# A streaming encoder layer: x arrives transposed, its split carries the norm's weight, and the row roots are applied where products leave PSUM

## The chip, the core and the metric

One core of one Trainium2 chip runs the whole layer. The metric is device microseconds (us) of one execution. Engines are named as in the profile: PE (matmuls), PEld (its weight loads), ACT (ScalarE), DVE (VectorE), POOL (GpSimd), and SP, whose queue issues all transfers.

## The reference, cut to what matters

```python
def rmsnorm(x, g):
    return x * lax.rsqrt(jnp.mean(x * x, -1, keepdims=True) + EPS) * g

def layer_inputs(x, norm_g, w_in, b_gate, qn_g, kn_g):      # x: 2048 prompt rows, and 64 sample rows
    h = rmsnorm(x, norm_g) @ w_in                           # (rows, 1024) @ (1024, 6144)
    qa, ka, va, za, qb, kb, vb, zb, ga, gb = split(h)       # ten column blocks
    qa, ka = rmsnorm(qa per 64, qn_g), rmsnorm(ka per 64, kn_g)
    ...
```

After it come differential attention over chunks (for the sample rows over a cache of 4096 frames), a retention branch, gates, three more projections and the residual add. Everything is fp32 in and out, and keys, values and states are outputs too.

Two facts make the change possible. The root of the norm is one factor per row of x, so it can be taken after the product: (r · x · g) @ W = r · ((x · g) @ W). And a product that is normalised again (qa, ka) loses the factor r anyway, if the eps in the second norm is scaled by 1/r².

## The kernel before

**Precision.** Each fp32 operand is split into a high and a low part in a rounded format (`xh`, `xl` for x, `wh`, `wl` for weights), and a product is three matmuls: high·high, high·low, low·high.

**Stages.** x is worked in two halves of 1024 prompt rows. Of a half, `xh` and `xl` hold the transposed, normalised x in two segments (tiles `xh0`/`xl0` and `xh1`/`xl1`) of 512 columns; the second segment of half 0 has 64 columns more for the sample rows. The contraction of 1024 is eight chunks of 128. `w_stream` walks over the column blocks of `w_in`: in half 0 the values (`va`), keys and queries, each as one group of 512 columns, then 256-column groups of the retention inputs and gates. Blocks that are needed with rows on partitions come from `natural` (x is the stationary operand); those needed transposed from `transposed` (the weights are). A coroutine per product (`fin_va`, `fin_qk`, `fin_vb`, `fin_t`) empties its PSUM bank.

**Order.** The code is a small planner. Coroutines with priorities yield until a planned PE time or until a buffer is free, and so fix the order in which PE, ACT and DVE get their instructions; projections fill the time in which attention waits. Each engine runs its queue strictly in that order. POOL and SP are ordered by the compiler's scheduler. SP has at most eight transfers in flight: each waits for the one eight before it.

**x before.** `x_prep` loads 128 rows of x as one tile `xt` of 128x1024. ACT squares and sums a row (L329), ACT and DVE form the inverse root (L335 to L350), and DVE multiplies the tile with the root and with the norm's weight row (L359). That row is spread over the partitions by a matmul with ones (`spread`, L308) in half 0 and by a transfer in half 1. `x_tile` then transposes the tile: eight 128x128 transposes on PE (L389) into two banks (`tp`, `pv`), a high part by ACT (L396) and a low part by DVE (L397). There are 17 such tiles. `opening` mixes the first of them with the first product by the list `OPENING` (matmuls of L578), and the others between the chunks of the values' group (L520, and L516 for the sample rows).

**Weights.** A piece is loaded to `ws`, ACT makes `wh` (L474), POOL makes `wl` (L484), for three early pieces DVE does (L481).

Of the kernel before, what the change touches and what calls it, by code (L numbers as in the profile page):

```python
# [43 lines left out]
XFLY = (3, 5)  # L44
# [4 lines left out]


OPENING = [(k[0], int(k[1])) for k in ("H0 X0 H1 X1 H2 X2 L0 H3 X3 L1 H4 X4 L2 T1 H5 X5 L3 H6 X6 L4 "
                                       "H7 X7 L5 L6 L7").split()]
# [12 lines left out]
class Hybrid:  # L65
    def __init__(self, tc, ins, outs):
        self.tc = tc
        self.nc = tc.nc
        self.i = ins
        self.o = outs  # L70
        self.pe = self.act = self.dve = self.pool = self.dma = 0.0
        self.tasks = []
        self.seq = 0
        self.res = {k: Res(n) for k, n in BUFS.items()}
        self.res["row"] = Res(ROWS)
        self.live = {"z": 0, "w": 0, "r": 0, "m": 0}
        self.done = set()
# [61 lines left out]
    def ld(self, dst, src, nbytes=0):  # L139
        self.nc.sync.dma_start(dst, src)  # L140
        self.dma = max(self.dma, self.pe) + nbytes / 300.0
        return self.dma + DMA_LAT
# [31 lines left out]
    def consts(self):  # L174
# [6 lines left out]
        yield lambda: len(self.xt_ready) > 8  # L181
# [34 lines left out]
        le = c("le", [128, 2])  # L216
        nc.scalar.activation(le, ls, AF.Exp)
        lam = c("lam", [128, 1])
# [43 lines left out]
    def x_prep(self, half):  # L262
        self.xq = []
        self.xin = []
        self.xfly = 0
        gn = jk = tg = None
        if half:
            yield from self.take("row", 2)
            gn, jk = self.row("gn"), self.row("xjk")
        else:  # L270
            yield from self.take("row")
            jk = self.row("xjk")
        tiles = self.xtiles(half)
        left = [len(tiles)]
        for j, (src, r, seg, col) in enumerate(tiles):
            yield lambda: self.xfly < XFLY[half] and (half > 0 or j < 2 or self.wloads >= 8)
            self.xfly += 1
            yield from self.take("row")
            xt = self.row("xt")[:r]
            self.xq.append(None)  # L280
            tx = self.ld(xt, src, 4096 * r)
            if j == 0 and half == 0:
                yield from self.take("row")
                gz = self.row("gz")
                self.nc.vector.memset(gz[:, :512], 0.0)
                self.nc.gpsimd.memset(gz[:, 512:], 0.0)
                tg = self.ld(gz[0:1, :], self.i["norm_g"][0:1, :], 4096)
                self.ld(self.ident, self.i["c_ident"], 1 << 16)
                gn = [self.psum("s") for _ in range(2)]
                self.gz = (gz, tg)  # L290
            elif j == 0:
                tg = self.ld(gn, self.i["norm_g"][0].partition_broadcast(128), 1 << 19)
            self.xin.append([xt, jk, gn, tx, tg, r, seg, col, left])
            if half:
                self.spawn(self.x_norm(j), 1, "w")
            yield self.pe
        yield lambda: left[0] == 0
        if half == 0:
            self.give("s", self.dve + LAT, 2)
        self.give("row", self.dve + LAT, 1 + half)  # L300

    def spread(self):

        gz, t = self.gz
        self.until(t)
        for k, ps in enumerate(self.xin[0][2]):
            yield from self.take("s")
            self.nc.tensor.matmul(ps, self.ones, gz[:, 512 * k:512 * k + 512], start=True, stop=True)  # L308
            t = self.P(2048)
        self.give("row", t)  # L310
        self.warm(2)
        self.xin[0][4] = t
# [10 lines left out]
    def norm_sums(self, j):  # L323

        nc = self.nc
        xt, jk, gn, t, tg, r, seg, col, left = self.xin[j]
        st = self.sp.tile([128, 3], F32, tag="x_st", name="x_st")
        ss, ms, y = (st[:r, k:k + 1] for k in range(3))
        nc.scalar.activation(jk[:r], xt, AF.Square, accum_out=ss)  # L329
        self.xin[j] += [ss, ms, y, self.A(1024, max(self.pe, t), 190)]  # L330

    def norm_log(self, j):
        nc = self.nc
        ss, ms, y, t = self.xin[j][9:]
        nc.scalar.activation(y, ss, AF.Ln, scale=1.0 / D, bias=self.epst[:y.shape[0]])  # L335
        nc.scalar.activation(y, y, AF.Exp, scale=-0.5)
        self.A(1, 0, 100)
        self.xin[j].append(self.A(1, 0, 40))

    def norm_mean(self, j):  # L340
        ss, ms, y, t = self.xin[j][9:13]
        self.nc.vector.tensor_scalar(ms, ss, 1.0 / D, EPS, op0=ALU.mult, op1=ALU.add)
        self.V(100, t)

    def norm_root(self, j):
        nc = self.nc
        ss, ms, y, t, t2 = self.xin[j][9:]
        nc.vector.tensor_scalar(ms, y, y, ms, op0=ALU.mult, op1=ALU.mult)
        nc.vector.tensor_scalar(ms, ms, -0.5, 1.5, op0=ALU.mult, op1=ALU.add)
        nc.vector.tensor_scalar(y, y, ms, 128.0 if isinstance(self.xin[j][2], list) else 1.0,  # L350
                                op0=ALU.mult, op1=ALU.mult)
        for _ in range(3):
            self.V(60, t2)

    def norm_scale(self, j):
        xt, jk, gn, tx, tg, r, seg, col, left, ss, ms, y, t, t2 = self.xin[j]
        for k, g in enumerate(gn if isinstance(gn, list) else [gn]):
            sl = slice(512 * k, 512 * k + g.shape[1])
            self.nc.vector.scalar_tensor_tensor(out=xt[:, sl], in0=xt[:, sl], scalar=y, in1=g[:r],  # L359
                                                op0=ALU.mult, op1=ALU.mult)  # L360
        self.xq[j] = (xt, self.V(1300, max(t2, self.xin[0][4])), r, seg, col)
        left[0] -= 1

    def x_norm(self, j):
        yield self.xin[j][3]
        self.norm_sums(j)
        self.norm_log(j)
        ss, ms, y, t, t2 = self.xin[j][9:]
        yield t
        self.norm_mean(j)  # L370
        yield t2
        self.norm_root(j)
        if self.xin[0][4] > self.pe:
            yield self.xin[0][4]
        self.norm_scale(j)

    def x_tile(self, j, wait=True, mid=None):
        nc = self.nc
        yield lambda: len(self.xq) > j and self.xq[j] is not None
        xt, t, r, seg, col = self.xq[j]  # L380
        if wait:
            yield t
        self.until(t)
        for q in range(2):
            tag = "tp" if q == 0 else "pv"
            yield from self.take(tag)
            tp = self.psum(tag)
            for c in range(4):
                nc.tensor.transpose(tp[:, c * r:(c + 1) * r],  # L389
                                    xt[:, (4 * q + c) * 128:(4 * q + c + 1) * 128],  # L390
# [1834 lines left out]
```

## Time and profile before

| | |
|---|---|
| time, three runs | 1954.27, 1958.63, 1959.08 us (median 1958.63) |
| the profiled execution | 1957.16 us, its span 1955.4 us, granted TensorE clock 0.997 |
| PE busy | 1936.0 us, 99% of the span |
| DVE, ACT, POOL busy | 1068.5, 1021.7, 476.0 us (55%, 52%, 24%) |
| moved by DMA | 303.86 MB, 155 GB/s in the mean |
| first product's first matmul | at 10.10 us |
| first matmul of the second column group (keys) | at 68.06 us |

The page gives busy times of one execution. In a row of the timeline stand the start, the busy time (the time over all, where x2 or more were merged), the engine, the line, the operation and its shape; in brackets is the idle time before it and what ended that. Matmuls overlap in the pipeline, so the distance of two starts, and not the busy time of one, says what a matmul costs PE.

### The profile page before, as it was taken

Reading aid. Unit: us, or ns where it says so; the run is one execution under the profiler, and the core shown is the slowest. Engines: PE = TensorE matmul, PEld = TensorE weight load, DVE = VectorE, ACT = ScalarE, POOL = GpSimd, SP = SyncE. Lnnn points to the kernel's source line nnn. Section 1 sums busy time; section 2 is a strip of 40 time slices with the busy share of each in tenths; the row PEclk is TensorE's granted clock in tenths of the full one; section 3 lists DMA queues with packets and bytes.
Section 4 is the critical chain, followed back from the end, with each engine's and each line's share of the span. In section 5 each row is a group of like instructions: output and inputs, shape, how many; then the busy total and the mean of one; then the engine's idle time right before and its main releaser. Section 6 shows DMA issues by size and latency. Waiting matters only on the chain.

```text
span 1955.4 us, 34054 instructions
## 1 busy us (share of the span) xinstructions
PE 1936.0 (99%) x12070; PEld 1740.5 (89%) x12070; DVE 1068.5 (55%) x2642; ACT 1021.7 (52%) x2220; POOL 476.0 (24%) x427
## 2 busy tenths in 40 slices
PE   9999999999999999999999999999999999999999
PEld 7878999999988989999998888888888899998887
DVE  6553665535565326546857656634753257545653
ACT  6432776645544436435766656644763545653321
POOL 2310211212121221222111211121122355543422
PEclk9999999999999999999999999999999999999999
DMA  7647554335656756664343342462233668866651
GB/s 250 210 130 197 150 162 116 119 86 159 181 162 170 174 137 209 197 202 136 111 130 95 103 136 83 130 182 91 73 98 111 208 201 261 258 197 196 189 156 59
DMA packets 367917, 303.86 MB, mean 155 GB/s; under 512 B 75137, under 2 KB 332417, under 8 KB 367746
## 3 DMA queue, kind: packets, MB, share of 16 engines
q1 hardware_dynamic: 367746, 301.68, 52.5%
q8 instruction: 95, 1.56, 0.3%
q14 instruction: 76, 0.62, 0.1%
HBM read 196.40 MB, written 100.14 MB: 152 GB/s over the span
## 4 chain that ended last, share of the span: by engine, by line
PE 91%; DVE 3%; DMA 3%; ACT 1%; issue 1%; SPq 1%; POOL 1%; ACTq 0%; DVEq 0%; POOLq 0%
PE mm L520 53%; PE mm L1882 4%; PE s L1000 3%; PE s L1001 3%; PE at L1108 3%; PE at L1882 2%; PE pv L1088 2%; PE pv L1087 2%; PE pv L1086 2%; PE mm L1670 1%; PE mm L1672 1%; PE mm L1671 1%; PE s L1671 1%; PE s L1672 1%; PE s L1670 1%; PE s L1882 1%
## 5 line engine op out<-in xcount | busy, mean ns | idle before, releaser
L520 PE MATMUL mm<-xh,wh 128*128 128x512 f32 (+2 forms) x1280 | 459.1, 359 | 0.0
L484 POOL TENSOR_TENSOR wl<-ws,wh 128x512 fp32r<-128x512 f32 x189 | 256.2, 1368 | 814.0 <-ACT wh L474 628.1
L520 PE MATMUL mm<-xh,wl 128*128 128x512 f32 (+2 forms) x1280 | 452.3, 353 | 0.0
L520 PE MATMUL mm<-xl,wh 128*128 128x512 f32 (+2 forms) x1280 | 451.7, 353 | 0.0
L520 PEld LDWEIGHTS mm<-xh,wl 128*128 128x128 f32 x1280 | 241.0, 188 | 31.6
L520 PEld LDWEIGHTS mm<-xh,wh 128*128 128x128 f32 x1280 | 241.3, 189 | 29.0 <-issue 0.2
L520 PEld LDWEIGHTS mm<-xl,wh 128*128 128x128 f32 x1280 | 241.5, 189 | 27.9
L520 PE MATMUL mm<-wh,xh 128*128 128x256 f32 (+1 forms) x824 | 258.4, 314 | 1.9 <-DVE tlo L757 1.7
L520 PE MATMUL mm<-wh,xl 128*128 128x256 f32 (+1 forms) x824 | 253.4, 308 | 0.0
L520 PE MATMUL mm<-wl,xh 128*128 128x256 f32 (+1 forms) x824 | 253.2, 307 | 0.1
L1123 DVE TENSOR_TENSOR atl<-at,ath 128x512 fp32r<-128x512 f32 (+1 forms) x144 | 93.8, 660 | 162.5 <-ACT ath L1121 162.5
L814 ACT COPY ev<-mm 128x512 f32<-128x512 f32 x140 | 71.4, 510 | 191.2 <-PE mm L520 177.9
L520 PEld LDWEIGHTS mm<-wh,xh 128*128 128x128 f32 x824 | 156.8, 190 | 11.6 <-DVE tlo L757 2.1
L520 PEld LDWEIGHTS mm<-wl,xh 128*128 128x128 f32 x824 | 156.9, 190 | 9.1 <-POOL wl L484 0.3
L520 PEld LDWEIGHTS mm<-wh,xl 128*128 128x128 f32 x824 | 156.8, 190 | 8.0
L1039 ACT ACTIVATE row<-row,a_mx 128x1024 f32<-128x1024 f32 (+7 forms) x160 | 153.9, 963 | 12.9 <-DVE a_mx L1019 12.5
L1009 DVE CUSTOM_DVE_ANT_0 row<-s,dfar 128x512 f32<-128x512 f32 (+2 forms) x192 | 118.5, 630 | 54.5 <-PE s L1001 53.9
L474 ACT CAST wh<-ws 128x512 fp32r<-128x512 f32 x192 | 116.1, 619 | 46.3 <-PE mm L520 18.5
L1121 ACT CAST ath<-at 128x512 fp32r<-128x512 f32 (+1 forms) x144 | 78.9, 563 | 104.9 <-PE at L1108 96.9
L1000 PE MATMUL s<-K,q 128*128 128x512 f32 (+3 forms) x320 | 118.6, 374 | 1.4 <-DVE a_acc L1009 1.4
L1001 PE MATMUL s<-K,q 128*128 128x512 f32 (+3 forms) x320 | 115.2, 363 | 0.5 <-DMA q<-qT 0.5
L1061 DVE SCALAR_TENSOR_TENSOR row<-row,a_w 128x1024 f32<-128x1024 f32 (+4 forms) x96 | 103.5, 1084 | 13.5 <-ACT row L1058 13.3
(301 smaller groups left out, 4077.8 us busy)
## 6 DMA issues: line engine op xcount, KB each, us to landing
ws<-in_w_in_dram SPq DMA_DIRECT2D x192, 256.0 KB, 3.0
q<-qT SPq DMA_DIRECT2D x128, 128.0 KB, 3.1
V<-vN SPq DMA_DIRECT2D x24, 512.0 KB, 5.3
K<-kT SPq DMA_DIRECT2D x48, 256.0 KB, 4.2
a<-mT SPq DMA_DIRECT2D x34, 256.0 KB, 4.0
gt<-gaT SPq DMA_DIRECT2D x64, 132.0 KB, 3.1
gt<-gbT SPq DMA_DIRECT2D x64, 132.0 KB, 3.1
mT<-gt SPq DMA_DIRECT2D x64, 132.0 KB, 2.9
```

Of the source, the lines that this page charges most:

```text
L474: self.nc.scalar.copy(h, st)
L484: self.nc.gpsimd.tensor_sub(l, st, h.bitcast(F32))
L520: nc.tensor.matmul(ps, p, q, start=c == 0 and i == 0, stop=c == KC - 1 and i == 2)
L814: nc.scalar.copy(ev, ps)
L1000: nc.tensor.matmul(ps, q1s, kk, start=True, stop=False)
L1001: nc.tensor.matmul(ps, q2s, kk, start=False, stop=True)
L1009: nc.vector.tensor_tensor_reduce(out=units[k0 // 1024][:, k0 % 1024:k0 % 1024 + n], in0=ps, in1=tab, scale=-SLOPES[h], scalar=3.0e38, op0= ...
L1039: nc.scalar.activation(u, u, AF.Exp, bias=mx, scale=-1.0, accum_out=lp[:, k:k + 1])
L1061: nc.vector.scalar_tensor_tensor(out=u0, in0=u0, scalar=w[:, 0:1], in1=u1, op0=ALU.mult, op1=ALU.add)
L1121: nc.scalar.copy(ah[:, :w], at[:, :w])
L1123: nc.vector.tensor_sub(al[:, :w], at[:, :w], ah[:, :w].bitcast(F32))
L1882: nc.tensor.matmul(q[b], u, v, start=fresh and c == 0 and m == 0, stop=c == 3 and m == 2, skip_group_check=True)
```

## The change

1. The host hands in `x_T` and `xs_T`, x transposed. `x_in` loads pieces of 128 contraction rows by 512 tokens (32 loads of 256 KB in place of 16 of 512 KB), the sample rows as one strip of 128x8x64. The norm's weight is loaded once as `gx`, eight numbers per partition.
2. `x_chunk` splits a piece directly: ACT writes `xh` as piece times `gx` (L297), DVE writes `xl` as piece times `gx` minus `xh` (L299). PE transposes nothing for x. For the sample strip `x_joint` has POOL square and scale it (L320, L322), then copy it into `xs`.
3. `x_square` sums squares over the chunks into `xacc` (ACT L309, DVE L312). `x_cols` (PE L414, matmuls with one column) turns them into one root per partition, `rs`, and an eps scaled by 1/r²; `x_root` (PE L374, ones times `xacc`) into the same roots along the free axis, `rsb`.
4. Where products leave PSUM the roots come in: `fin_va` and `fin_vb` scale by `rs`, `fin_qk` takes only the scaled eps, `fin_t` multiplies by `rsb`. `fin_t` was a copy on ACT (L814, L816) and is now a multiplication on DVE (L872, L874). All of them wait for their roots (`roots`, `self.tb`).
5. The opening is new: four row tiles of segment 0 are accumulated side by side in four banks (`mm`, `mm`, `s`, `s`), chunk by chunk, as pieces of x and of the weights land; then three of segment 1 in `at`, `at`, `pv`; then the last tile and the sample rows in `s`. The wide `fin_va` keeps its high and low parts in one `row` buffer. Of the first eight weight pieces only the first gets its low part from DVE.
6. In half 1 all eight pieces of a segment are split as soon as half 0 has done with that segment.

The core of the diff:

```diff
-                nc.tensor.transpose(tp[:, c * r:(c + 1) * r],
-                                    xt[:, (4 * q + c) * 128:(4 * q + c + 1) * 128],
-                                    self.ident[:r, :r])
...
+        nc.scalar.activation(hi, raw, AF.Identity, scale=g)                       # x_chunk
+        nc.vector.scalar_tensor_tensor(out=lo, in0=raw, scalar=g, in1=hi.bitcast(F32),
+                                       op0=ALU.mult, op1=ALU.subtract)
...
+        nc.scalar.activation(out, raw, AF.Square)                                 # x_square
+            nc.vector.tensor_add(acc[:, :512], acc[:, :512], out)
...
+        nc.gpsimd.tensor_mul(tmp, raw, raw)                                       # x_joint
+        nc.gpsimd.tensor_mul(raw, raw, self.gx.unsqueeze(2).to_broadcast([128, KC, 64]))
...
+            for i, (x, w, ready) in enumerate(((xh, h, max(th[seg, c], tw)), (xl, h, self.xr[seg][c]), (xh, l, t))):
+                for k, (tag, ps) in enumerate(pss):                               # opening
+                    nc.tensor.matmul(ps, x[:, 128 * k:128 * k + 128], w, start=c == 0 and i == 0,
+                                     stop=c == KC - 1 and i == 2)
...
-            nc.scalar.copy(ev, ps)                                                # fin_t
+            nc.vector.tensor_mul(ev, ps, rsb)
...
-        if n in (5, 7, 8):                                                        # w_low
+        if n == 1:
             self.nc.vector.tensor_sub(l, st, h.bitcast(F32))
```

What that does to the engines' queues is seen at three places. On PE at the start of the program, before (`mm_215` is the bank of the first product, `wh_175` the first weight piece, `xt_121` the first tile of x):

```order
L320 MATMUL at_106<-ones_102 128x128 x8
L308 MATMUL s_128<-gz_123,ones_102 128x512
L308 MATMUL s_129<-gz_123,ones_102 128x512
L320 MATMUL at_160<-ones_102 128x128 x2
L389 MATMUL tp_168<-ident_101,xt_121 128x128 x4
L389 MATMUL pv_179<-ident_101,xt_121 128x128 x4
L578 MATMUL mm_215<-wh_175,xh0_115 128x512
L578 MATMUL mm_215<-wh_175,xl0_116 128x512
```

and in the changed kernel:

```order
L440 MATMUL at_110<-ones_106 128x128 x8
L604 MATMUL mm_123<-wh_172,xh0_119 128x512
L604 MATMUL mm_124<-wh_172,xh0_119 128x512
L604 MATMUL s_125<-wh_172,xh0_119 128x512
L604 MATMUL s_126<-wh_172,xh0_119 128x512
L604 MATMUL mm_123<-wl_173,xh0_119 128x512
```

Between the first eight matmuls, which only warm the array, and the first product nothing is left; each weight piece now meets four row tiles (the last row shown is the ninth product matmul, the first with the low weights).

On POOL at the same place. Before, the low parts of chunks 3 and 5 (`ws_138`, `ws_142`; DVE makes those of chunks 4, 6 and 7), and right behind them those of the keys' pieces:

```order
L484 TENSOR_TENSOR wl_197<-ws_138,wh_196 128x512
L484 TENSOR_TENSOR wl_201<-ws_142,wh_200 128x512
L484 TENSOR_TENSOR wl_447<-ws_440,wh_446 128x512
L484 TENSOR_TENSOR wl_511<-ws_442,wh_510 128x512
L484 TENSOR_TENSOR wl_515<-ws_444,wh_514 128x512
```

and in the changed kernel, where `ws_149`, `ws_152`, `ws_155` are the pieces of chunks 5, 6 and 7, and `xt_267` is the strip of sample rows:

```order
L510 TENSOR_TENSOR wl_240<-ws_149,wh_239 128x512
L320 TENSOR_TENSOR xt_267<-xt_267 128x512
L322 TENSOR_TENSOR xt_267<-xt_267,gx_104 128x512
L510 TENSOR_TENSOR wl_280<-ws_152,wh_279 128x512
L510 TENSOR_TENSOR wl_280<-ws_155,wh_279 128x512
L510 TENSOR_TENSOR wl_339<-ws_189,wh_338 128x512
```

The two operations on the strip now stand ahead of the low parts of chunks 6 and 7, which POOL makes too. On SP the strip's load stands behind all 16 pieces of half 0's x and 11 weight pieces; before, the sample rows' load stood behind 8 tiles of x and 11 weight pieces.

On PE where half 0 ends (`wh` as second operand is a gate group of half 0; `xh_8737` is x of half 1), before:

```order
L520 MATMUL mm<-xh_117,wl 128x320
L389 MATMUL tp<-ident,xt 128x128 x4
L389 MATMUL pv<-ident,xt 128x128 x4
L1457 MATMUL at<-rvx,rqk 128x128 x4
L520 MATMUL mm<-xh_117,wh 128x320
```

and in the changed kernel (`xh_8697` is x of half 1):

```order
L550 MATMUL mm<-xl_122,wh 128x320
L550 MATMUL mm<-xh_121,wl 128x320
L374 MATMUL tp<-xacc,ones 128x512
L550 MATMUL mm<-wh,xh_8697 128x256
L550 MATMUL mm<-wl,xh_8697 128x256
```

The sixteen groups of four transposes of half 1 are gone; two matmuls with ones and two sets of four one-column matmuls take their place.

559 lines of the change are left out of this document (315 added, 244 removed).

## The prediction

> **What bounds the kernel now.** I read the page's busy times first, then its chain that ended last, then the timeline of PE in the opening.
>
> ```profile
> PE 1936.0 (99%) x12070; PEld 1740.5 (89%) x12070; DVE 1068.5 (55%) x2642; ACT 1021.7 (52%) x2220; POOL 476.0 (24%) x427
> PE 91%; DVE 3%; DMA 3%; ACT 1%; issue 1%; SPq 1%; POOL 1%; ACTq 0%; DVEq 0%; POOLq 0%
> ```
>
> PE is busy for 99% of the span and carries 91% of the chain. So the time is the sum of what PE is given, plus its few waits, and an edit counts by what it takes from PE's queue or adds there. Where PE isn't filled is the opening:
>
> ```profile
> 10.10 0.50 PE L578 MATMUL mm<-wh,xh 128*128 128x512 f32 x1 [1.27 <-ACT wh L474]
> 22.03 0.60 PE L389 MATMUL tp<-ident,xt 128*128 128x128 f32 x4
> 22.46 0.60 PE L389 MATMUL pv<-ident,xt 128*128 128x128 f32 x4
> 22.82 0.48 PE L520 MATMUL mm<-wh,xh 128*128 128x512 f32 x1
> 23.13 0.39 PE L520 MATMUL mm<-wl,xh 128*128 128x512 f32 x1
> 23.06 5.58 PE mm L520 x24
> 64.39 0.39 PE L516 MATMUL mm<-wh,xs 128*128 128x512 f32 x1
> 68.06 0.40 PE L520 MATMUL mm<-wh,xh 128*128 128x512 f32 x1
> ```
>
> The sixth row is from the chain: 24 matmuls of 512 columns take 5.58, so one costs 0.2325. The values' group has 8 x 24 + 16 = 208 of them, 48.4 us of work. The keys start at 68.06 (last row). The opening thus costs 68.06 - 48.4 = 19.7 us beyond its work: the wait for x, its norm and the first weights, and nine tiles of transposes.
>
> **The change, part by part.** The sum goes by the profiled execution, 1957.16 us; the median of the runs, 1958.63, is 1.5 above it, and I carry the difference over.
>
> *(a) First matmul.* These rows price it:
>
> ```profile
> 0.73 0.40 SPq L140 DMA_DIRECT2D xt<-in_x_prompt_dram  x1
> 4.15 1.06 ACT L329 ACTIVATE xjk<-xt 128x1024 f32<-128x1024 f32 x1 [2.14 <-DMA xt<-in_x_prompt_dram]
> DMA to landing us min/median/max: 3.7/3.7/3.7
> L474 ACT CAST wh<-ws 128x512 fp32r<-128x512 f32 x192 | 116.1, 619 | 46.3 <-PE mm L520 18.5
> L721 ACT ACTIVATE thi<-tp,gq 128x512 fp32r<-128x512 f32 x16 | 11.1, 693 | 14.1 <-PE tp L711 9.3 <-DMA qT<-thi 4.8
> ```
>
> The first load landed 3.4 us after its issue. The third row is the gate bias `bg`, which is fetched as `gx` is, in single floats, and twice as many: 3.7. So x's first piece and `gx` are there by 4.4 to 4.8, ACT needs 0.69 for `xh` and 0.62 for `wh`, and PE starts at about 6.1 (5.5 to 7). SP then issues 16 loads where it issued 10; the pieces land faster than PE uses them (a chunk of x and weights is 512 KB, PE takes 12 x 0.2325 = 2.79 us for it, that is 188 GB/s; the rows under (c) show twice that).
>
> *(b) The wait that is added: POOL.* The low weights of chunks 6 and 7 stand behind two operations on the sample strip. What lands when:
>
> ```profile
> 15.87 0.56 SPq L140 DMA_DIRECT2D xt<-in_x_sample_dram  x1
> xt<-in_x_sample_dram SPq DMA_DIRECT2D x1, 256.0 KB, 8.2
> 10.12 7.33 POOL L484 TENSOR_TENSOR wl<-ws,wh 128x512 fp32r<-128x512 f32 x5 [8.87 <-ACT wh L474]
> ```
>
> The sample rows landed at 15.87 + 8.2 = 24.1. Ahead of them went 8 x 512 + 11 x 256 = 6,912 KB; ahead of the strip go 16 x 256 + 11 x 256, the same. I take 24.1. Three POOL operations (square, scale, low part of chunk 6) at 7.33/5 = 1.47 end at 28.5. PE wants that low part at 6.1 + 6 x 2.79 + 8 x 0.2325 = 24.7: it waits 3.8 us, and everything behind it on PE with it. Bounds: if the strip lands after the first load's 3.4, at 19.3, POOL is ready at 23.7 and the wait is 0; if its 256-byte runs cost `bg`'s 3.7 on top, it lands at 27.8 and the wait is 7.5. The nearest row is the sample rows' own.
>
> *(c) The clock.* After such a wait the array may run at half speed:
>
> ```profile
> 9.00:10.00 1.00, 0.00 (x0) 0.00 (x0) 0.59 (x2) 1.00 (x4) 0.00 (x0) 1.00 1.04 393
> 11.00:12.00 1.00, 0.48 (x2) 0.30 (x2) 0.90 (x5) 1.00 (x3) 0.86 (x2) 1.00 1.06 418
> 12.00:13.00 1.00, 1.00 (x6) 0.78 (x5) 1.00 (x2) 1.00 (x3) 1.00 (x2) 0.83 1.06 424
> 13.00:14.00 1.00, 1.00 (x4) 0.81 (x3) 1.00 (x2) 1.00 (x4) 1.00 (x1) 0.50 1.01 401
> 14.00:15.00 1.00, 1.00 (x4) 0.81 (x3) 1.00 (x2) 0.59 (x2) 1.00 (x2) 0.50 1.00 401
> 15.00:16.00 1.00, 1.00 (x5) 0.70 (x5) 1.00 (x1) 0.00 (x0) 1.00 (x2) 0.50 1.07 426
> ```
>
> Behind the busy times of the five engines stand the granted clock, the share of DMA and GB/s. The clock was 0.50 from 13 to 16 and 0.83 in the microsecond before. PE had done nothing from 9 to 10 (1.27 us in all, by its row above) and was busy for 0.48 us of 11 to 12. The loss was 0.17 + 3 x 0.5 = 1.7 us. A wait of 3.8 is longer than both gaps together, so I add 1.7 (bounds 0 and 1.7). The Trainium skill ("TensorE: Matmul & The Clock Gate", Part 1: The HAM clock gate) says that the clock halves after about one idle window of 3.4 us, in windows that run freely. The trace is stricter: no idle time there reached 3.4. By that rule a wait of 3.8 would often not hold a whole window, and the sum below would be 1.7 better.
>
> *(d) End of the values' group.* Segment 0 ends at 28.5 + 16 x 0.2325 + 1.7 = 33.9. Then come 72 matmuls of three tiles, 24 of the last tile, 16 of the sample rows: 112 x 0.2325 = 26.0. New on PE are the matmuls for the roots:
>
> ```profile
> 4.62 2.48 PE L308 MATMUL s<-gz,ones 128*128 128x512 f32 x4
> 536.25 0.31 PE L520 MATMUL mm<-xh,wl 128*128 128x320 f32 x1
> 536.39 0.28 PE L1317 MATMUL s<-s_l,fold 128*128 128x2 f32 x2
> 536.53 0.39 PE L520 MATMUL mm<-xh,wh 128*128 128x320 f32 x1
> 536.76 0.31 PE L520 MATMUL mm<-xl,wh 128*128 128x320 f32 x1
> 751.16 0.60 PE L389 MATMUL tp<-ident,xt 128*128 128x128 f32 x4
> 751.60 0.60 PE L389 MATMUL pv<-ident,xt 128*128 128x128 f32 x4
> 751.96 0.36 PE L520 MATMUL mm<-xh,wh 128*128 128x256 f32 x1
> 752.16 0.28 PE L520 MATMUL mm<-xl,wh 128*128 128x256 f32 x1
> 752.27 0.28 PE L520 MATMUL mm<-xh,wl 128*128 128x256 f32 x1
> ```
>
> Two fp32 matmuls of 512 columns took 2.48: 1.24 each. An fp32 matmul with a narrow operand took 536.53 - 536.39 = 0.14, and the next start came 0.08 late: four in a row about 0.6. Two sets of four and one wide one fall into this stretch: 2.4. The keys start at 33.9 + 26.0 + 2.4 = 62.3, **5.8 earlier** than 68.06.
>
> *(e) Behind it.* One wide root matmul (1.24), one of 64 columns and one narrow one (0.5 by the same rows) follow among the keys: **-1.7**. In half 1 a tile's transposes go from 751.16 to 751.96 and cost the next start 0.08, 0.88 in all; eight tiles 7.0. Two sets of four (1.2) and two wide ones (2.5) come in: **+3.3**. Half 0's nine tiles are within (d).
>
> *(f) What I cost at nothing.* `fin_t`, moved to DVE:
>
> ```profile
> L814 ACT COPY ev<-mm 128x512 f32<-128x512 f32 x84 | 49.1, 585 | 130.5 <-PE mm L520 123.4 <-issue 6.0 <-DMA ws<-in_w_in_dram 1.0
> L679 DVE TENSOR_TENSOR raw<-mm,gk 128x512 f32<-128x512 f32 x16 | 11.0, 689 | 26.3 <-ACT sq L673 26.3
> ```
>
> A bank is emptied in 0.69 in place of 0.59, while the next group holds PE for 5.58 (24 matmuls) in the other `mm` bank; that bank is the cover, and without it each of the 140 groups would cost 0.7 and the release. In half 0, x's splits, squares and sums run beside 2.79 us of PE per chunk: ACT 0.69 + 0.62 + 0.6. The doubled loads of half 1, four pairs of them waiting on SP for a split, lie beside other projections. Scaled copies in `fin_va` and the small eps operations (0.2 to 0.3 each) lie beside matmuls as their predecessors do.
>
> Sum: 5.8 - 1.7 + 3.3 = 7.4. 1957.16 - 7.4 = 1949.8; on the scale of the median 1951.2, that is 0.38% faster.
>
> **The rivals.**
>
> *A: no wait at POOL.* If the strip lands by 20, 3.8 and 1.7 are not lost: 1951.2 - 5.5 = 1945.7. For it: a lone load takes 3.4. Against it: the sample rows' 8.2 with the same bytes ahead.
>
> *B: DVE paces the first segment.* Two operands in SBUF while POOL runs:
>
> ```profile
> L481 DVE TENSOR_TENSOR wl<-ws,wh 128x512 fp32r<-128x512 f32 x3 | 4.8, 1640 | 0.0
> L1766 DVE TENSOR_TENSOR bl<-wst,bh 128x512 fp32r<-128x512 f32 x12 | 10.6, 885 | 4.0 <-ACT bh L1763 3.9
> ```
>
> The same subtraction took 1.64 beside POOL in the opening and 0.89 later. `xl` and the sum into `xacc` have two such operands: 3.28 per chunk against PE's 2.79, 3.9 us over eight chunks. With POOL's wait this is covered; without it, 1945.7 + 3.9 = 1949.6. The Trainium skill ("GPSIMD Engine Reference", Key points) names this: POOL shares its SBUF interfaces with VectorE and contends with instructions that have two SBUF inputs. The two rows agree.
>
> *C: no net gain.* The roots of segment 1 come only after its squares, and eight banks are then held; behind the sample rows' end at 62.3 ACT's queue holds a copy, four evacuations of two scaled copies, three operations for roots, three casts and the first square of the keys: 0.6 + 5.5 + 1.8 + 1.9 + 0.6, so that this bank is free at 73.4 with DVE's 0.69. PE wants it for the third tile of the keys at 62.3 + 1.7 + 2 x 5.58 = 75.2. That is a margin of 2 us with no wait of ACT for a store in it; 7 us more of such waits would give 1951.2 + 5 = 1956, within the noise.
>
> *D: slower.* `fin_t` queues on DVE behind attention's long operations, and PE waits for `mm`. With 256-column groups the other bank covers only 24 x 0.11 = 2.6 us (752.27 - 752.16). It decides from 13.3 us in all (7.4 + 5.9), 0.095 per group. If 40 groups lose 0.4 each: 16 us, 1967. Against it: DVE is at 55%, and the stretch in which it is busiest, 81%, holds no such group (second row: ACT's L814 alone, x0):
>
> ```profile
> 900.00:1000.00 100.00, 100.00 (x778) 96.86 (x777) 81.19 (x232) 70.27 (x142) 11.95 (x10) 1.00 0.40 121
> 900.00:1000.00 100.00, 0.00 (x0) 1.00 0.40 121
> ```
>
> **How the numbers follow.** A measurement of this kernel can tell about 0.3%, 5.9 us, from no change. Forecast 0.50, A 0.15, B 0.05, C 0.18, D 0.12. The forecast's own range is 1946 (a wait of nearly 0, and full clock) to 1955 (a wait of 7.5); about two thirds of its chance lie below 1952.7, the bound of "faster". Faster: 0.34 + 0.15 + 0.05, 0.54. Same: the rest of the forecast and C, 0.34. Slower: D, 0.12. The range runs from 1945 to 1959: it leaves out most of D and little below A.
>
> **What would show it.** (a) The first product's matmul near 6.1. (b) POOL idle until the strip lands near 24, and PE waiting for `wl` for some 4 us at about 25. (c) Granted clock 0.50 for up to 3.4 us behind that. (d) The keys' first matmul near 62. (e) No transposes of x near 750, PE still at 99% there. (f) No PE wait on `fin_t`. The forecast is wrong if PE waits on DVE or ACT releases of `mm` for more than a few us in all, or if the strip lands early.

## The result, and the profile after

The changed kernel takes 1990.87 us (median of four runs, 1988.93 to 1991.52), the kernel before 1958.86 (four runs beside them): ratio 1.0166, interval 1.0148 to 1.0184. It is 32 us slower; 7 us faster were forecast. The profiled execution took 1991.33, its span 1989.2, at a mean granted clock of 0.990 (before 0.997).

The page's busy times and its chain that ended last:

```profile
PE 1945.8 (98%) x11970; PEld 1739.0 (87%) x11970; DVE 1172.3 (59%) x2806; ACT 968.5 (49%) x2080; POOL 485.5 (24%) x429
PE 82%; DMA 6%; DVE 4%; issue 2%; ACT 2%; POOL 2%; SPq 1%; POOLq 0%; ACTq 0%; DVEq 0%
```

PE has 100 matmuls less and is busy for 10 us more; time at half clock, worked out below, is more than that. And it carries 82% of the chain in place of 91%; the shares of DMA, DVE, ACT and POOL have grown. To see where, PE's busy time and the granted clock by stretches, first of the kernel before, then of the changed one (columns: the stretch, its length, PE busy and its matmuls, clock, share of DMA, GB/s):

```profile
0.00:70.00 70.00, 66.99 (x313) 0.98 0.72 249
70.00:200.00 130.00, 129.71 (x706) 1.00 0.59 168
200.00:760.00 560.00, 558.13 (x3600) 1.00 0.55 152
760.00:960.00 200.00, 198.31 (x1629) 1.00 0.53 162
960.00:1500.00 540.00, 538.53 (x3163) 1.00 0.38 113
```

```profile
0.00:70.00 70.00, 59.55 (x240) 0.93 0.62 196
70.00:200.00 130.00, 122.30 (x589) 0.96 0.55 167
200.00:760.00 560.00, 553.03 (x3558) 1.00 0.54 150
760.00:960.00 200.00, 194.72 (x1531) 0.98 0.56 170
960.00:1500.00 540.00, 539.94 (x3229) 1.00 0.39 113
```

Idle time is length less busy time. Over the program it is 1955.4 - 1936.0 = 19.4 us before and 1989.2 - 1945.8 = 43.4 after: 24.0 more. Of these, 7.4 are added up to 70 us, 7.4 from 70 to 200, 5.1 from 200 to 760, 3.6 from 760 to 960. The clock adds (1 - 0.990) x 1989.2 - (1 - 0.997) x 1955.4 = 14.0 (with these rounded clocks, so an estimate to within 2 us). Together 38.0, against a growth of the span by 33.8: PE's work at full clock fell by some 4. So PE did become lighter, as forecast, and lost 38 to waits and to the clock that waits cost.

The waits, in PE's timeline of the opening (start, busy, engine and line, idle time before and its releaser):

```profile
6.45 0.72 PE L604 MATMUL mm<-wh,xh 128*128 128x512 f32 x2 [1.95 <-ACT wh L500]
29.77 0.74 PE L604 MATMUL mm<-wl,xh 128*128 128x512 f32 x2 [2.79 <-POOL wl L510]
56.72 0.50 PE L550 MATMUL s<-wh,xh 128*128 128x512 f32 x1 [2.81 <-ACT raw L797]
64.44 0.48 PE L546 MATMUL s<-wh,xs 128*128 128x512 f32 x1 [1.84 <-ACT raw L797]
70.64 0.39 PE L550 MATMUL mm<-wh,xh 128*128 128x512 f32 x1
84.08 0.37 PE L414 MATMUL tp<-ones,xt 128*64 128x1 f32 x2 [4.12 <-DVE xroot L387]
85.40 0.63 PE L550 MATMUL mm<-wh,xl 128*128 128x512 f32 x1
85.83 0.63 PE L550 MATMUL mm<-wh,xh 128*128 128x512 f32 x1
105.91 0.50 PE L550 MATMUL mm<-wh,xh 128*128 128x512 f32 x1 [2.48 <-DVE raw L703]
```

The first product starts at 6.45, POOL's wait is there, and yet the keys start at 70.64 (fifth row), not near 62. PE stood for the bank `s` twice, for 2.81 us up to 56.7 and for 1.84 up to 64.4. The longest wait is among the keys: 4.12 for the one `tp` bank. Behind it matmuls of 512 columns start every 0.43 us (85.40, 85.83), not every 0.23: half clock.

Who holds these banks? ACT in the same place, from its first emptying of segment 1 to the freeing of `tp`:

```profile
74.09 0.67 ACT L790 ACTIVATE vhl<-at,rs 128x512 fp32r<-128x512 f32 x1
75.78 0.69 ACT L797 ACTIVATE raw<-at,rs 128x512 f32<-128x512 f32 x1 [1.01 <-DVE vhl L792]
76.36 0.68 ACT L790 ACTIVATE vhl<-at,rs 128x512 fp32r<-128x512 f32 x1
77.86 0.69 ACT L797 ACTIVATE raw<-at,rs 128x512 f32<-128x512 f32 x1 [0.82 <-DVE vhl L792]
82.62 0.68 ACT L381 ACTIVATE xroot<-tp,epst 128x512 f32<-128x512 f32 x1
83.33 0.69 DVE L387 TENSOR_SCALAR xroot<-tp 128x512 f32<-128x512 f32 x1 [1.33 <-DMA vN<-vhl]
```

ACT writes the high part (L790), stands still while DVE writes the low part (L792), then copies the output (L797). The first bank takes 76.36 - 74.09 = 2.3 us, four take 82.62 - 74.09 = 8.5. The root's first operation (L381) is queued behind them, DVE's L387 behind that, and PE's next root matmul needs the same bank. One of ACT's waits between L790 and L797 was three times as long as the others, on a bank `mm` of segment 0. The row roots themselves stood ahead of the low part in DVE's queue (L391 to L396, 48.89 to 53.1), and the first `s` was emptied only behind that, for the 56.7 above.

```profile
48.89 1.79 DVE L391 TENSOR_TENSOR xroot<-xroot,xacc 128x512 f32<-128x512 f32 x1
53.06 0.74 DVE L792 SCALAR_TENSOR_TENSOR vhl<-mm,rs,vhl 128x512 fp32r<-128x512 f32 x1
53.83 0.69 ACT L797 ACTIVATE raw<-mm,rs 128x512 f32<-128x512 f32 x1 [2.99 <-DVE vhl L792]
```

So three things meet: the order in which a bank is emptied, the time at which emptying can begin, and engines that work strictly in order.

That time is late. Segment 1's squares (L309) run here:

```profile
38.44 0.20 ACT L232 ACTIVATE sm_y<-ep 128x4 f32<-128x4 f32 x1 [12.70 <-DVE ep L419]
56.56 1.14 ACT L309 ACTIVATE xacc<-xt 128x512 f32<-128x512 f32 x2
66.96 0.63 ACT L309 ACTIVATE xacc<-xt 128x512 f32<-128x512 f32 x1 [0.76 <-DVE xacc L312]
```

They start at 56.56 and end at 67.6; the roots of segment 1 follow, and its banks are emptied from 74.09. The first three had been full since PE came to the bank `s`, at 56.7 - 2.8 = 53.9. Yet ACT had stood idle for 12.7 us before 38.44, in front of the first segment's roots.

### The profile page after: what moved, and what is told of

Same layout as the page of the kernel before. It is cut to its first block, busy times and chain, and to the rows that moved or that the text cites. A ratio compares the mean times of both kernels' runs of the same rounds, so it can differ in the third digit from the quotient of the medians.

```text
span 1989.2 us, 33871 instructions
## 1 busy us (share of the span) xinstructions
PE 1945.8 (98%) x11970; PEld 1739.0 (87%) x11970; DVE 1172.3 (59%) x2806; ACT 968.5 (49%) x2080; POOL 485.5 (24%) x429
## 4 chain that ended last, share of the span: by engine, by line
PE 82%; DMA 6%; DVE 4%; issue 2%; ACT 2%; POOL 2%; SPq 1%; POOLq 0%; ACTq 0%; DVEq 0%
PE mm L550 47%; PE mm L1941 4%; PE s L1059 3%; PE s L1060 3%; PE at L1167 3%; PE at L1941 2%; PE pv L1147 2%; PE pv L1146 2%; PE pv L1145 2%; PE s L1941 1%; DMA qT<-thi 1%; SPq L135 1%; PE s L1730 1%; POOL wl L510 1%; DMA xt<-in_x_T_dram 1%
## 5 line engine op out<-in xcount | busy, mean ns | idle before, releaser
L550 PEld LDWEIGHTS mm<-xl,wh 128*128 128x128 f32 x1280 | 241.4, 189 | 28.5
L550 PE MATMUL mm<-wh,xh 128*128 128x256 f32 (+1 forms) x768 | 239.7, 312 | 7.4 <-ACT raw L797 4.9
L550 PE MATMUL mm<-wh,xl 128*128 128x256 f32 (+1 forms) x768 | 233.9, 305 | 0.3 <-DVE xl L299 0.3
L550 PE MATMUL mm<-wl,xh 128*128 128x256 f32 (+1 forms) x768 | 234.0, 305 | 0.1
L550 PEld LDWEIGHTS mm<-wh,xh 128*128 128x128 f32 x768 | 148.5, 193 | 16.6 <-ACT raw L797 5.7
L872 DVE TENSOR_TENSOR ev<-mm,rsb 128x512 f32<-128x512 f32 x140 | 83.0, 593 | 133.1 <-PE mm L550 121.1
L550 PEld LDWEIGHTS mm<-wl,xh 128*128 128x128 f32 x768 | 148.6, 193 | 7.4 <-issue 0.5
L550 PEld LDWEIGHTS mm<-wh,xl 128*128 128x128 f32 x768 | 148.3, 193 | 6.4 <-DVE xl L299 0.5
L943 POOL TENSOR_TENSOR r_y<-r_y,r_sq 128x256 f32<-128x256 f32 x33 | 25.7, 777 | 335.9 <-DVE r_sq L940 211.6
```

Of the source, the lines that this page charges most:

```text
L550: nc.tensor.matmul(ps, p, q, start=c == 0 and i == 0, stop=c == KC - 1 and i == 2)
L872: nc.vector.tensor_mul(ev, ps, rsb)
```

## The experiments

Four theories: (1) PE waits for banks that ACT and DVE empty late, because of the order within a bank and of squares and roots in the same queues; (2) POOL's wait for the sample strip drives the loss; (3) `fin_t` on DVE does (rival D of the prediction); (4) emptying the banks sets the pace by itself, whatever the norm does. All ratios are to the kernel before. In the edited kernels some lines move by a few: the low part and the copy of `fin_va` are L796 and L793, the opening's matmuls L605.

**1. The order within a bank (raw_first).** In `fin_va`:

```diff
                 nc.scalar.activation(hi[:, sl], ps[:, sl], AF.Identity, scale=sc)
-                nc.vector.scalar_tensor_tensor(out=lo[:, sl], in0=ps[:, sl], ...)
                 nc.scalar.activation(raw[:, sl], ps[:, sl], AF.Identity, scale=sc)
+                nc.vector.scalar_tensor_tensor(out=lo[:, sl], in0=ps[:, sl], ...)
```

> The changed kernel with one order turned round: where a values' bank is emptied, ACT makes the high part and the output copy one behind the other, and DVE the low part after both; in the changed kernel ACT's copy stands behind DVE's low part and ACT idles for it (0.82 to 0.97 us, eight times in the opening; 0.55 for each narrow one). Theory 1 (PE waits for banks that ACT empties too late, and each wait costs a stretch of half clock as well): the wait of 4.1 for `tp` at 84 shrinks to about 1, the two waits for `s` (2.8, 1.8) and the two at 899 and 915 (3.0, 1.3) become smaller, and one or two stretches of half clock go: 1991 falls by 8 to 15, to about 1979. Theory 2 (the loss is POOL's wait for the sample strip and what follows from it) and theory 3 (it is `fin_t` on DVE): within 3 of 1991.

Measured: 1974.65 (1970.01 to 1978.92), ratio 1.0083 [1.0061, 1.0104]. Two operations exchanged give back 16 us, half of the loss. The wait of 4.12 for `tp` fell to 0.66, that for `s` at 64.4 to 1.20, and that for `s` at 56.7 went; half clock before 200 us fell from six stretches of 3.4 us to two. POOL's wait is longer here, 4.24 in place of 2.79.

**2. Roots taken as known (const_roots).**

```diff
-        yield lambda: len(self.rst[half]) > j
-        ...
-        return self.rs[:, half, j:j + 2], self.ep_[:, half, j:j + 2]
+        return self.rsc[:, 0:2], self.rsc[:, 2:4]          # constants
```

> The changed kernel with the row roots taken as known: the emptying of values and keys reads constants and waits for no root (the norm's factor of the values and the scaled eps are left out of the result); sums, root matmuls and everything else stay. Theory 1 (banks held by late roots): PE's waits for `s` (2.8 and 1.8), for `tp` (4.1) and for the keys' bank (2.5) go, 11 us, and with them four or five stretches of half clock at 1.7 each: 1991 falls by 14 to 20, to about 1974. Theories 2 (POOL's wait) and 3 (`fin_t` on DVE): within 3 of 1991.

Measured: 1990.46, ratio 1.0170 [1.0149, 1.0191]: nothing in the total. But the opening became faster, and the loss moved behind it. The keys start at 62.92:

```profile
62.92 0.40 PE L550 MATMUL mm<-wh,xh 128*128 128x512 f32 x1
77.55 1.87 PE L414 MATMUL tp<-ones,xacc 128*128 128x1 f32 x8 [3.48 <-DVE xacc L312]
```

Banks emptied early push the squares back: PE now stands 3.48 us before a root matmul whose sums aren't done. Even so it is 12.7 us ahead among the keys: their first matmul of sample rows (`mm<-wh,xs`, L546) starts at 118.7, in the changed kernel at 131.4. Most of that is lost again at one place: a wait of 6.87 that ends at 206.1 and 6.8 us at half clock behind it (3.4 lost), 10.3 in all. PE wants a tile there that DVE has not normalised, and DVE had stood idle for 16.66 us in front of a `tlo` buffer that a store still held. So the expectation (1974) was not met, but the total doesn't show that late roots cost nothing. Experiment 9 meets the same wait and shows its rows.

**3. The strip's work deferred (strip_late).** `x_joint` yields until segment 0's products are planned.

> The changed kernel, but the work on the sample strip (POOL's square and scaling) begins only when the first segment's products are done, so that POOL has nothing ahead of the low weights of chunks 6 and 7. Theory 2 (POOL's wait drives the loss): the wait of 2.8 at 30 and its stretch of half clock go, the opening's later waits with them, and 1991 falls by 10 or more. Theory 1 (late banks): the 2.8 and 1.7 go, but the banks are emptied no sooner, so that a part comes back as a wait for `s` or `tp`: 1991 falls by 0 to 5, to about 1988. Theory 3 (`fin_t`): within 5 as well.

Measured: 1989.82, ratio 1.0159 [1.0133, 1.0184]. The edit didn't do what it says: POOL's queue is ordered by the compiler, and the strip's two operations still stood ahead of the last two low parts:

```profile
26.34 1.04 POOL L320 TENSOR_TENSOR xt<-xt 128x512 f32<-128x512 f32 x1 [8.21 <-DMA xt<-in_xs_T_dram]
27.46 1.04 POOL L322 TENSOR_TENSOR xt<-xt,gx 128x512 f32<-128x512 f32 x1
28.46 2.49 POOL L510 TENSOR_TENSOR wl<-ws,wh 128x512 fp32r<-128x512 f32 x2
```

It tells nothing of theory 2; experiment 6 does.

**4. `fin_t` on ACT (fin_t_act).** `nc.vector.tensor_mul(ev, ps, rsb)` became `nc.scalar.copy(ev, ps)`, and the scaled form likewise.

> The changed kernel with the transposed products emptied by ACT as before the change (a copy, or a copy with a scale; the row roots are left out of them), so that DVE has 140 operations of 0.59 us less and ACT as many more. Theory 3 (rival D: `fin_t` on DVE holds up PE): 1991 falls by 15 or more, to 1975 or below. Theories 1 and 2: within 4 of 1991.

Measured: 1987.17, ratio 1.0146 [1.0129, 1.0163], an interval that overlaps the changed kernel's. Theory 3 falls: at most a few us lie there. The group in the changed kernel agrees: of DVE's 133.1 us idle in front of it 121.1 ended with PE's matmuls, and in that profile PE never waits for L872.

```profile
L872 DVE TENSOR_TENSOR ev<-mm,rsb 128x512 f32<-128x512 f32 x140 | 83.0, 593 | 133.1 <-PE mm L550 121.1 <-DMA obT<-rru 3.5 <-DMA vc<-in_cache_v_diff_dram 3.1
```

**5. The same order in the kernel before (before_lo_first).** There, `tensor_sub(lo, ...)` was put ahead of `scalar.copy(raw, ps)`.

> The kernel before, with one order turned the other way: where a values' bank is emptied, DVE's low part stands ahead of ACT's output copy, as in the changed kernel. Theory 1a (the order costs by itself, wherever it stands): the old kernel loses about as much as the changed one won by the turn, 16 us, to 1974. Theory 1b (the order costs only where several banks wait for ACT together, which the roots bring about; in the old kernel the banks come one every 5.6 us): within 4 of 1958.

Measured: 1962.48, ratio 1.0011 [1.0001, 1.0021]: 2 us. The order is nearly free where banks come one every 5.6 us. In the changed kernel, where banks wait for their roots and then come together, it costs 16.

**6. The strip on DVE (raw_dve).** From here on the base is raw_first.

```diff
-        nc.gpsimd.tensor_mul(tmp, raw, raw)
+        nc.vector.tensor_mul(tmp, raw, raw)                # x_joint, behind the first roots
...
-        nc.gpsimd.tensor_mul(raw, raw, self.gx...)
+        nc.vector.tensor_mul(raw, raw, self.gx...)
```

> The changed kernel with the copy ahead of the low part (1974.7), and the strip's square and scaling on DVE, behind the first segment's roots, so that POOL has only weights ahead of the low parts of chunks 6 and 7. Theory 1 (banks and ACT's order): PE's wait of 4.2 at 29 and its stretch of half clock (1.7) go; the roots of the first segment hang on squares and not on POOL, so most of it is kept: 1969 to 1971. Theory 2 (the strip drives the loss): 1965 or below. If the wait is hidden anyway: 1974 as in the base.

Measured: 1976.15, ratio 1.0079 [1.0064, 1.0094], the same as its base. POOL's wait is gone, and PE gave all of it back at the next bank:

```profile
53.25 0.75 DVE L796 SCALAR_TENSOR_TENSOR vhl<-s,rs,vhl 128x512 fp32r<-128x512 f32 x1 [0.98 <-ACT raw L793]
54.06 0.79 PE L550 MATMUL s<-wh,xh 128*128 128x512 f32 x1 [5.21 <-DVE vhl L796]
```

The bank `s` is free at 54.0 here and at 53.3 in the base, whether PE comes at 48.9 (here) or at 53.4 (in the base, late by POOL's wait). So the expected 1969 to 1971 was not reached, and theory 2 is not the cause here; the wait that I forecast at POOL was covered by a later one that I hadn't seen.

**7. Two other suspects (raw_joint_late, raw_one).** The first puts the sample rows' root matmuls later into PE's order, the second empties a narrow values' bank in one operation per engine.

> The changed kernel with the copy ahead of the low part (1974.7), and the sample rows' two root matmuls put some 10 and 20 us later into PE's order. In the base PE stands 0.7 and 2.2 us in front of them while ACT and DVE work off the values' banks, and 3.4 us at half clock follow. If these waits are what they look like: 2.9 + 1.7 go, 1970. If PE is held there by the same backlog through the keys' banks: within 2 of 1974.7, with a new wait on a keys' bank in the trace.

> The changed kernel with the copy ahead of the low part (1974.7), and a values' bank of two row tiles emptied in one operation of 512 columns each on ACT and DVE in place of two of 256 (the second tile gets the first one's roots; that is left out of the result). If the doubled operations of the narrow banks hold PE where half 1 begins (waits of 3.8 in all near 885, 1.7 before the change, and a stretch of half clock): 1971. If that wait is the stores' and not the operations': within 2 of 1974.7.

Measured: 1976.55, ratio 1.0075 [1.0060, 1.0090], and 1977.18, ratio 1.0082 [1.0067, 1.0097]. Neither moves the time. With the root matmuls moved, their waits left the trace, and new ones on `tp` for the keys' own transposes (2.1 and 1.1 us) came in.

**8. Squares of segment 1 first (raw_dve_sq).** In `opening`, on top of experiment 6:

```diff
-            while ahead < min(16, n + (2 if n < KC - 1 else 4)):
+            while ahead < min(16, n + (2 if n < KC - 1 else 6)):
...
+            if n == KC - 1:
+                for k in range(KC):
+                    yield lambda: len(self.xraw[0, 1]) > k
+                    square(1, k)
...
-                if seg:
-                    self.spawn(squares(), 1, "w")
```

> The changed kernel with the copy ahead of the low part and the strip's work on DVE (1976), and with the squares of segment 1 moved ahead: right behind those of segment 0, where ACT and DVE stand idle for 7.6 and 5.4 us until PE has the first sums, in place of behind the emptying of the first banks. Nothing is left out. Theory 1 (the opening is paced by ACT and DVE working off squares, roots and banks in a row, while they idled earlier): the wait of 5.2 for `s` and one or two waits among the keys go, and the time falls to about 1966. Theory 4 (the emptying of the banks by itself sets the pace, whenever the roots are there): within 3 of 1976.

Measured: 1961.14 (ten runs, 1956.78 to 1964.42), ratio 1.0003 [0.9991, 1.0015]: the loss is gone. The opening of its profiled execution (span 1954.9):

```profile
6.43 1.22 PE L605 MATMUL mm<-wh,xh 128*128 128x512 f32 x2 [1.60 <-ACT wh L500]
35.27 0.95 PE L414 MATMUL tp<-ones,xacc 128*128 128x1 f32 x8
36.08 0.71 PE L605 MATMUL at<-wl,xh 128*128 128x512 f32 x2
61.37 0.40 PE L550 MATMUL mm<-wh,xh 128*128 128x512 f32 x1
```

After the start PE waits for nothing up to the keys, which begin at 61.37, 6.7 us earlier than before the change. ACT and DVE do the same work as in experiment 6, in another order. (Its start is slow: matmuls of 512 columns are 0.43 apart up to 12.5, which the clock column can't show, as its record begins at 12.53.)

**9. Known roots with the order turned (raw_const_dve).** const_roots on top of experiment 6.

> The changed kernel with the copy ahead of the low part and the strip's work on DVE (1976), and with the row roots taken as known where banks are emptied (the norm's factor of the values and the scaled eps are left out of the result; the sums and root matmuls stay). Theory 1: as roots alone gained nothing with the old order (1990.5 against 1991), it is the work and not the waiting; what is left is the squares' work among the keys: 1970 to 1976. Theory 5 (with the order turned, late roots are what holds `s` for 5.2): 1967 or below.

Measured: 1971.92, ratio 1.0058 [1.0038, 1.0078], 4 us less than its base and within what theory 1 expected. That is luck: up to 185 us the trace shows what theory 5 says (its execution took 1976.88, among the slowest of seven).

| profile | PE idle, 7 to 185 us | first `mm<-wh,xs` of the keys |
|---|---|---|
| changed kernel | 15.2 | 131.4 |
| const_roots (experiment 2) | 8.3 | 118.7 |
| raw_dve (experiment 6, the base) | 9.2 | 118.7 |
| raw_const_dve (this one) | 1.8 | 106.9 |
| raw_dve_sq (experiment 8) | 0.3 | 109.6 |

The wait for `s` is gone, although segment 1's squares still run late (L309 up to 65.7) and in the same queues. Then one wait takes back what was won:

```profile
180.53 8.60 SPq L140 DMA_DIRECT2D qT<-tlo  x1
193.59 0.75 DVE L749 SCALAR_TENSOR_TENSOR tlo<-tp,gq,thi 128x512 fp32r<-128x512 f32 x1 [19.70 <-DMA qT<-tlo]
197.10 0.66 PE L738 MATMUL tp<-ident,raw 64*128 64x64 f32 x4 [9.91 <-DVE raw L723]
```

A store of `tlo` holds SP for 8.60 us behind the loads of keys and values for attention; DVE stands 19.70 us for the buffer, PE 9.91 us for DVE, and 10.2 us at half clock follow (5.1 lost). Experiment 6 has no wait of PE there above 1 us. So known roots gain some 12 us up to the keys' sample rows, in the old order of the emptying (131.4 to 118.7) and in the new (118.7 to 106.9), no less than the earlier squares do (118.7 to 109.6). Why the store falls behind those loads in these two runs was not tried.

**10. No norm at all (no_norm, raw_no_norm).** `x_square`, `x_cols`, `x_root` issue nothing.

> The changed kernel without the norm's roots altogether (left out: squares, their sums, root matmuls, roots; constants stand in their place, and the same operations empty the banks). PE has 7.4 us less to do (five sets of root matmuls at 0.8 and as many at 0.9, less for the sample rows), ACT 24 us and DVE 30 us over the program. Theory 1 (squares and roots on ACT and DVE crowd the opening): beside the 7.4 the waits behind them go, some 10 us with their half clock: about 1972. Theory 4 (the emptying alone): 1984, the 7.4 only.

> The same with the copy ahead of the low part, base 1974.7. Theory 1: 7.4 less for PE and some 8 us of waits and half clock among the values and keys: 1958 to 1960, as the kernel before. Theory 4: with the order turned nothing is left to gain but the 7.4: 1967.

Measured: 1946.71, ratio 0.9921 [0.9903, 0.9938], and 1945.29, ratio 0.9913 [0.9895, 0.9931]. Both are lower than either theory expected: without squares and roots the order within a bank is worth 1.4 us, within the intervals. So theory 4 falls too: the emptying doesn't set the pace by itself, in neither order. It is the norm that makes the order cost. Whether by the late date of its roots or by its work in the same two queues, these two runs can't tell, since they leave out both; experiment 9 speaks for the date.

**11. Which edit does what (sq_early, raw_sq).** The move of the squares alone, and with the order turned but the strip on POOL.

> The changed kernel with the squares of segment 1 moved ahead, and nothing else (old order of the emptying, the strip on POOL). Theory 1a (the late squares alone cause the loss): as with all three edits, about 1961. Theory 1b (the two add: late squares some 15, the order some 15): about 1976. Theory 1c (the order costs only while ACT is crowded; with the squares out of the way it costs little, as in the kernel before): 1961 to 1967, plus POOL's wait of 3 to 4 and its half clock, which is now no longer hidden: 1964 to 1971.

> The changed kernel with the copy ahead of the low part and the squares of segment 1 moved ahead; the strip stays on POOL. Where POOL's wait was hidden behind the wait for `s` (1974.7 with it, 1976 without), it should now stand open, since that wait is gone: 4.2 and a stretch of half clock (1.7) above the kernel with all three edits, 1967. If it is still hidden: 1961.

Measured: 1980.12, ratio 1.0094 [1.0078, 1.0110], above all three expectations and nearest to 1b, and 1966.25, ratio 1.0030 [1.0019, 1.0040], where POOL's wait stands open (3.1 us in its profile), as expected.

| edits to the changed kernel | ratio | us above before (ratio x 1959) |
|---|---|---|
| none | 1.0166 | 32.5 |
| order | 1.0083 | 16.3 |
| squares | 1.0094 | 18.4 |
| order, strip | 1.0079 | 15.5 |
| order, squares | 1.0030 | 5.9 |
| order, squares, strip | 1.0003 | 0.6 |

Order and squares nearly add up: 16.2 + 14.1 = 30.3 expected, 26.6 found. The strip is worth 0.8 (within the intervals) while a bank's wait covers it and 5.3 once nothing does, about the 3.8 + 1.7 that the prediction gave it.

**12. What is left near 870 us (best_row).** With all three edits, narrow values' banks take their buffers from `row`.

> All three edits (1961), and the narrow values' banks put their high and low parts in one buffer of the pool `row`, as the wide ones do, in place of `thi` and `tlo`, which they share with the stores of the queries. If the wait of 3.0 and 1.0 at 871 and 886 is that of those buffers: 1957. If rows are as scarce there: 1961 or above.

Measured: 1957.76 (ten runs, 1956.20 to 1962.51), ratio 0.9990 [0.9981, 1.0000]. Of experiment 8 and of this kernel, the stretch where half 1's values are emptied:

```profile
760.00:960.00 200.00, 195.87 (x1590) 1.00 0.55 168
```

```profile
760.00:960.00 200.00, 199.22 (x1624) 1.00 0.55 169
```

3.3 us of idle time went, as expected of those buffers. The ratio fell by 0.0013, 2.5 us, but the two intervals overlap. By its median it is the fastest version that computes everything; it can hardly be told from the kernel before.

## Why the prediction was wrong, point by point

**(a) The first matmul: right.** 6.45 against 6.1. At 7.4 a stretch of half clock began, which was not in the sum.

**(b), (c) POOL's wait and its half clock: right in kind, 2.8 in place of 3.8, from 27.0 to 29.8 in place of 24.7 to 28.5.** POOL sat for the strip as forecast:

```profile
25.88 1.17 POOL L320 TENSOR_TENSOR xt<-xt 128x512 f32<-128x512 f32 x1 [7.20 <-DMA xt<-in_xs_T_dram]
```

The strip landed at 25.8, not 24.1, and PE came later too. But the wait's price was taken as the loss of whoever waits first. Experiment 6 shows that it cost nothing as long as `s` was released late, experiment 11 that it costs 5.3 when `s` isn't. Of the six stretches of half clock before 200 us one followed POOL's wait (31.3 to 34.7), as forecast; the other five followed other waits.

**(d) The keys at 62.3: wrong by 8.3 (70.64); this step failed.** It counted PE's matmuls from 33.9 on and assumed that every bank is free when PE wants it; PE waited 2.81 and 1.84 us for `s`, with a stretch of half clock behind. The count itself was nearly right: in experiment 12, where PE neither waits for POOL nor starts at half clock, the keys start at 58.15, and the forecast without its 5.5 for POOL's wait gives 56.8. That experiments 8 (61.37) and 2 (62.92) land near 62.3 is luck: experiment 8 has no wait at POOL, but some 2.9 us lost to half clock at its start (its first 14 matmuls take 6.13 us) and 0.9 more for the root matmuls than the sum took.

**(e) Roots on PE, and half 1: right.** In experiment 8 four narrow matmuls held PE from 35.27 to 36.08, 0.81 against the 0.6 taken; a wide one cost 0.86 there (from 47.58 to 48.91, less two other matmuls) against 1.24. The transposes went. But half 1 gave nothing net, because idle time from 760 to 960 rose from 1.7 to 5.3 us.

**(f) Costed at nothing: this is where the time went.** I wrote that scaled copies in `fin_va` lie beside matmuls "as their predecessors do". Their predecessors were ACT, ACT, DVE; the new ones are ACT, DVE, ACT, which the diff shows and I did not read. With two readers in turn the bank takes 2.1 us of ACT's queue in place of about 1.4, the sum of its own two operations (0.67 and 0.69). The Trainium skill ("PSUM — Partial Sum Buffer", PSUM bank collisions raise a hardware error) says that two engines must not touch one bank at once, reads included, and that a dependency is put between them; the rows above agree with it (0.8 to 1.0 us idle before L797, `<-DVE vhl`; with the order turned DVE waits for ACT, 0.98 before L796). The same paragraph let the squares run beside PE's chunks at no cost. Those of segment 0 did; those of segment 1 are queued behind its last chunk and ran from 56.56 to 67.6, so that its roots, and with them its banks, came late. Experiments 1 and 11 give the two omissions 16 and 14 us, 26.6 together. `fin_t`, in the same paragraph, was costed rightly.

**The rivals.** C was the mechanism (late roots, eight banks held, ACT's backlog), with a price of 5 in place of some 30. I looked only at the third bank of the keys, found 2 us of margin, and put 5.5 us for four evacuations; they took 8.5. The first bank that PE lacked was `s`, 20 us earlier, and nothing in the sum stood for it. And in it I gave waits their length, without the half clock behind each. D was wrong in its place (experiment 4), A in its premise, and B's slow DVE rows were there but no PE wait followed from them in the first segment.

**What stays open.** PE's waits and clock from 1500 us on, in code that the change doesn't touch, are somewhat worse in the changed kernel: two stretches more of half clock. Their cause was not tried. And the forecast's gain of 7.4 was reached by none of the versions that compute everything. In experiment 8's profile PE is busy 4.9 us less than before (1931.1 against 1936.0) and idle 4.4 more (23.8 against 19.4); between 200 and 960 us alone it idles 5.2 more, and of that only the 3.3 of experiment 12 were traced to a cause. Experiment 10's gain of 14 us against experiment 8 is more than the some 7.5 us of root matmuls that PE is spared; in the two profiles it is 10.9, of which 2.9 are the slow start of experiment 8's.

## What to carry to other kernels

When a change moves work off the bound engine, price the queues that take it in the order in which they run, bank by bank: ask of every bank when its first and last reader come, and what stands ahead of them. A stretch in which the helpers idle (here 12.7 us of ACT before 38) is where their work belongs; moving eight squares there gave 14 us without shortening anything. A wait that you can remove is worth nothing while another one ends behind it: two edits at a time told what one could not. And a total that doesn't move can hide a gain and a loss: compare two traces at the same place in PE's order before you drop a theory.

## What was not expected of the hardware

**The clock halves after waits shorter than 3.4 us.** In the 17 profiles of this study, PE's idle gaps of 2.4 to 3.4 us were followed within 7 us by a stretch at half clock in 23 of 26 cases, those of 1.6 to 2.4 in 36 of 47, those of 1.2 to 1.6 in 4 of 31 (neighbouring gaps are not told apart in this count; of gaps with no other idle time over 0.4 us near them it was 13 of 15, 14 of 20 and none of 13). A stretch lasted 3.41 us or a multiple. The Trainium skill ("TensorE: Matmul & The Clock Gate", Part 1: The HAM clock gate) puts it down to at least one idle window of about 3.4 us; the length agrees, the threshold found here is lower. Within a trace the stretches begin on a grid of 3.413 us, to 0.01. Cut into windows on that grid, from 14 us on, all 17 traces together have 65 windows in which PE idled for 1.9 us or more, and half clock followed in the next window each time; of the 9,558 in which it idled for less than 1.0, 11 were followed by it (in between 20 of 85). So a gap of 2 us costs or doesn't by where it falls on the grid. The 4.12 of waiting at 84 so cost 4.1 and, with 5.2 us at half clock behind it (starts 0.43 apart up to 89.3), 2.6 more.

**A small DVE operation can take as long as a POOL operation.** Two of the same kind, with 4 and 8 elements per partition, and the POOL operations beside the first (beside the second there were none):

```profile
39.47 4.24 POOL L510 TENSOR_TENSOR wl<-ws,wh 128x512 fp32r<-128x512 f32 x3 [8.51 <-ACT wh L500]
42.51 1.22 DVE L237 TENSOR_TENSOR sm_t<-sm_t,ep 128x4 f32<-128x4 f32 x1
99.60 0.17 DVE L237 TENSOR_TENSOR sm_t<-sm_t,ms 128x8 f32<-128x8 f32 x1
```

1.22 us against 0.17. The chain of five such operations that makes the roots took from 41.24 to 44.2 because of two of them, in front of every bank of the first segment.
